# A small unread transfer as the first issue, and the first y load behind the opening barrier

## The chip, the cores and the metric

The kernel runs on one core of a Trainium2 chip. The metric is the device time of one execution in microseconds, the median of several. The span in a profile runs from the first instruction that the profile keeps to the last, and is some 1.6 us shorter than the device time. All runs told here were at a granted clock of 1.0; the program uses no TensorE.

## The reference

```python
x, y: 1024 x 4096 float32
return np.sum(np.abs(x - y), axis=-1)     # 1024 sums
```

33.55 MB are read and 4 KB are written.

## The kernel before

Each of the 128 partitions holds eight rows. Four rows of x (`xa`) and four of y (`yb`) come first, then three more rows of x (`xb`), then y rows into the places of `yb` that the subtractions have left free, and the last row in five pieces. VectorE subtracts in place, and ScalarE takes the absolute value and sums it with one instruction. The helper `put` places an instruction in the program's opening block. With `before="Drain"` it stands ahead of the issuing engine's part of the opening barrier, otherwise behind it.

```python
for r in (slice(0, 1), slice(1, H)):                     # SP, ahead of the barrier
    put(lambda: nc.sync.dma_start(out=xa[:, r, :], in_=xr[:, r, :]).then_inc(s_first, 16), before="Drain")
put(lambda: nc.scalar.dma_start(out=yb, in_=yr[:, 0:H, :]).then_inc(s_first, 16), before="Drain")   # ACT
put(lambda: nc.sync.dma_start(out=xb[:, 0:H - 1, :], in_=xr[:, H:K - 1, :]).then_inc(s_xb, 16))     # behind it
for k in range(H - 1):
    put(lambda: nc.sync.wait_ge(s_sub, k + 1))           # the subtraction of row k has freed yb[k]
    put(lambda: nc.sync.dma_start(out=yb[:, k, :], in_=yr[:, H + k, :]).then_inc(s_row[k], 16))
...                                                      # the last row, in pieces
# VectorE: the first subtraction waits for s_first >= 48, that is for all of xa and yb
...
put(lambda: nc.sync.wait_ge(s_end, n_part + 3))
put(lambda: nc.sync.dma_start(out=orr, in_=ro).then_inc(s_out, 16))
```

## Time and profile before

| | kernel before |
|---|---|
| device time, median of 6 beside the changed kernel | 84.59 us (84.42 to 84.68) |
| span of the profiled execution (84.33 us) | 82.7 us |
| DMA engines at work, mean of 16 | 95.6% of the span |
| VectorE, ScalarE busy | 44%, 38% |
| VectorE's first wait for data ends | 41.0 us |
| last reduction starts | 80.77 us |

The table says that the transfers bound the kernel: no compute engine is busy for half of the span. The views that show it, and the first microseconds in which the change acts, stand in the prediction. The end of the timeline of the kernel before (start us, length us, engine, line, what, and in brackets the idle time ahead and its releaser):

```profile
80.27 0.46 DVE L161 TENSOR_TENSOR last_piece<-xb_rows,yb_rows 128x288 f32<-128x288 f32 x1 [0.20 <-DMA yb_rows<-in_y_dram]
...
80.77 0.46 DVE L163 TENSOR_REDUCE ro_sums<-last_piece 128x1 f32<-128x292 f32 x1
```

The last subtraction starts when the last piece of y is there, and the reduction follows it directly. So the end hangs on the end of the stream.

### The profile page before, as it was taken

What the parts mean: (1) busy time and instruction counts of PE and PEld (TensorE: products, weight loads), DVE (VectorE), ACT (ScalarE), POOL (GpSimd) and SP (SyncE); (2) the same over time, 40 slices, a digit from 0 to 9 for tenths busy, and PEclk for the clock granted to TensorE, in tenths of its full rate; (3) what the DMA queues carried; (4) which work ended last, traced back from release to release, by engine and by line L of the source; (5) the groups of instructions that cost most, each with busy time, mean ns of one, the idle gap of its engine ahead of it and who ended that gap; (6) DMA issues with size and microseconds to landing.
All of it is one profiled execution on the core that took longest, in us unless ns stands there. A gap on an engine that the chain in (4) does not pass through costs nothing.

```text
span 82.7 us, 104 instructions
## 1 busy us (share of the span) xinstructions
DVE 36.3 (44%) x16; ACT 31.6 (38%) x27; POOL 0.2 (0%) x4
## 2 busy tenths in 40 slices
DVE  0000000000000000000199999999279898999682
ACT  3200000000000000000000979889790599999990
POOL 0000000000000000000000000000000000000000
DMA  4990992992998889988888999858999989999950
GB/s 127 634 634 24 610 634 87 547 634 127 507 507 380 380 380 547 594 380 380 380 380 380 452 618 452 380 254 380 483 404 436 452 380 431 414 411 413 404 209 2
DMA packets 2592, 33.56 MB, mean 406 GB/s; under 512 B 416, under 2 KB 928, under 8 KB 1696
## 3 DMA queue, kind: packets, MB, share of 16 engines
q1 hardware_dynamic: 2448, 25.17, 72.2%
q10 hardware_dynamic: 144, 8.39, 23.4%
HBM read 33.55 MB, written 0.00 MB: 406 GB/s over the span
## 4 chain that ended last, share of the span: by engine, by line
DMA 68%; DVE 22%; ACT 7%; ACTq 0%; SPq 0%; issue 0%
DMA xa_rows<-in_x_dram 49%; DMA yb_rows<-in_y_dram 19%; DVE xa_rows L127 16%; ACT xb_rows L132 7%; DVE xb_rows L127 5%; DVE ro_sums L163 1%; ACTq L199 0%; SPq L106 0%
## 5 line engine op out<-in xcount | busy, mean ns | idle before, releaser
L127 DVE TENSOR_TENSOR xa_rows<-xa_rows,yb_rows 128x4096 f32<-128x4096 f32 x4 | 17.4, 4420 | 41.0 <-DMA xa_rows<-in_x_dram 41.0
L132 ACT ACTIVATE xa_rows<-xa_rows 128x4096 f32<-128x4096 f32 x4 | 14.5, 3617 | 44.8 <-DVE xa_rows L127 44.8
L127 DVE TENSOR_TENSOR xb_rows<-xb_rows,yb_rows 128x2048 f32<-128x2048 f32 (+5 forms) x9 | 17.9, 2019 | 3.6 <-DMA yb_rows<-in_y_dram 3.5
L132 ACT ACTIVATE xb_rows<-xb_rows 128x2048 f32<-128x2048 f32 (+5 forms) x9 | 15.2, 1686 | 3.1 <-DVE xb_rows L127 3.0
L132 ACT ACT_TABLE_LOAD x1 | 1.3, 1283 | 1.3 <-PEq L185 1.3
L132 ACT ACTIVATION_READ_ACCUMULATOR xb_rows<-xb_rows 128x1 f32 x9 | 1.7, 186 | 0.0
L132 ACT ACTIVATION_READ_ACCUMULATOR xa_rows<-xa_rows 128x1 f32 x4 | 0.7, 186 | 0.0
L161 DVE TENSOR_TENSOR last_piece<-xb_rows,yb_rows 128x288 f32<-128x288 f32 x1 | 0.5, 458 | 0.2 <-DMA yb_rows<-in_y_dram 0.2
L163 DVE TENSOR_REDUCE ro_sums<-last_piece 128x1 f32<-128x292 f32 x1 | 0.5, 456 | 0.0
L155 DVE TENSOR_REDUCE ro_sums<-half_sums 128x2 f32<-128x4 f32 x1 | 0.1, 149 | 0.0
L185 POOL MEMSET const-bfloat16-1.0<- 128x1 bf16 x1 | 0.1, 101 | 0.0
L185 POOL MEMSET const-uint8-127<- 128x1 uint8 x1 | 0.1, 101 | 0.0
L185 POOL MEMSET const-float32-0.0<- 128x1 f32 x1 | 0.1, 98 | 0.2 <-issue 0.2
L185 POOL MEMSET const-float32-1.0<- 128x1 f32 x1 | 0.1, 98 | 0.0
## 6 DMA issues: line engine op xcount, KB each, us to landing
xa_rows<-in_x_dram SPq DMA_DIRECT2D x1, 6144.0 KB, 40.6
xb_rows<-in_x_dram SPq DMA_DIRECT2D x1, 6144.0 KB, 54.3
yb_rows<-in_y_dram SPq DMA_DIRECT2D x3, 2048.0 KB, 15.5
xa_rows<-in_x_dram SPq DMA_DIRECT2D x1, 2048.0 KB, 24.0
xb_rows<-in_x_dram SPq DMA_DIRECT2D x1, 864.0 KB, 17.8
yb_rows<-in_y_dram SPq DMA_DIRECT2D x1, 864.0 KB, 16.0
xb_rows<-in_x_dram SPq DMA_DIRECT2D x1, 528.0 KB, 16.9
yb_rows<-in_y_dram SPq DMA_DIRECT2D x1, 528.0 KB, 17.7
```

Source lines behind the costliest of these rows:

```text
L127: put(lambda: nc.vector.tensor_sub(out=tx, in0=tx, in1=ty).then_inc(s_sub, 1))
L132: put(lambda: nc.scalar.activation(tx, tx, ABS, accum_out=to).then_inc(sem, 1))
L155: put(lambda: nc.vector.reduce_sum(out=ro[:, K - 3:K - 1], in_=half, axis=AX).then_inc(s_end, 1))
L161: put(lambda: nc.vector.tensor_sub(out=last[:, n_part:n_part + w], in0=tx, in1=ty).then_inc(s_end, 1))
L163: put(lambda: nc.vector.reduce_sum(out=ro[:, K - 1:K], in_=last, axis=AX, apply_absolute_value=True).then_inc(s_end, 1))
L185: nc = _bacc.Bacc("TRN2", target_bir_lowering=False, num_devices=1)
```

## The change

The intent, as one reads it from the code, is to wake the DMA path with a transfer that nobody reads, so that the first large transfer behind it finds the path ready. It puts one descriptor of 512 bytes on each of the 16 DMA engines. At the same time ACT's y transfer moves behind the opening barrier.

```diff
+    probe = sbuf("probe", [16, 128])
+    s_probe = tc.alloc_semaphore("s_probe")
...
+    put(lambda: nc.sync.dma_start(out=probe, in_=xr[0:P:P // 16, 0, 0:128]).then_inc(s_probe, 16), before="Drain")
     for r in (slice(0, 1), slice(1, H)):
         put(lambda: nc.sync.dma_start(out=xa[:, r, :], in_=xr[:, r, :]).then_inc(s_first, 16), before="Drain")
-    put(lambda: nc.scalar.dma_start(out=yb, in_=yr[:, 0:H, :]).then_inc(s_first, 16), before="Drain")
+    put(lambda: nc.scalar.dma_start(out=yb, in_=yr[:, 0:H, :]).then_inc(s_first, 16))
...
+    put(lambda: nc.sync.wait_ge(s_probe, 16))
     put(lambda: nc.sync.wait_ge(s_end, n_part + 3))
```

## The prediction

> **What bounds the kernel now.** I read the page's queue part first, then the chain that ended last, then the first microseconds of the timeline, and last the same stretch by quarter microseconds. One row of the strip in slices and the two DMA queues of the kernel before:
>
> ```profile
> DMA  4990992992998889988888999858999989999950
> ...
> q1 hardware_dynamic: 2448, 25.17, 72.2%
> q10 hardware_dynamic: 144, 8.39, 23.4%
> ```
>
> The columns of the queues are packets, MB and share of 16 engines' time. 72.2% and 23.4% are 95.6% of the span of 82.7 us, so each of the 16 DMA engines is at work for 79.1 us. q1 holds what SP issues, q10 the one 8.39 MB y transfer that ACT issues. VectorE is busy 44% and ScalarE 38%. The chain of waits says the same (start us, us, what):
>
> ```profile
> 0.43 40.55 DMA xa_rows<-in_x_dram
> ...
> 41.00 13.11 DVE xa_rows L127 x3
> ...
> 54.13 16.08 DMA yb_rows<-in_y_dram
> ...
> 74.76 5.47 ACT xb_rows L132 x8
> ...
> 80.77 0.46 DVE ro_sums L163
> ```
>
> VectorE waits until 41.0 us for the first 16.8 MB (four rows of x and of y per partition, counted by one semaphore to 48), and then again and again for y rows. The stretch 41.00 to 54.11 is put down to VectorE only because its subtractions free the buffers for the later y rows. The DMA strip stays near full there: 6 MB of x were already queued behind the first x rows and keep the engines fed. So this is one gapless stream: about 1.0 us of start, 79.1 us of transfer, ending at 80.1 us, and VectorE's last wait for data indeed ends at 80.27 us. Then come the last subtraction (0.46 us), the last reduction and the store. ScalarE runs nearly without a gap from 64.98 to 80.75 us, so at the end it is almost level with the stream, but its work too comes at the stream's pace. Whatever moves the beginning of the stream moves the end by as much; whatever only changes the order in which x and y share the engines moves nothing, as long as there is always something queued.
>
> The timeline of the first microseconds (start, length, engine, line, what) is where the change acts:
>
> ```profile
> 0.00 0.85 SPq L106 DMA_DIRECT2D xa_rows<-in_x_dram  x2
> 0.12 0.36 ACTq L107 DMA_DIRECT2D yb_rows<-in_y_dram  x1
> ...
> 1.26 1.28 ACT L132 ACT_TABLE_LOAD   x1 [1.26 <-PEq L185]
> 1.26 0.33 SPq L108 DMA_DIRECT2D xb_rows<-in_x_dram  x1
> ```
>
> One issue occupies its sequencer for 0.33 to 0.47 us (SP's two are 0.38 by the chain and the rest of 0.85). The barrier lets SP and ACT go at 1.26 us, about 0.4 us after SP's second issue ended. Now the same stretch in windows; the last two columns are the DMA share and GB/s, and a packet is booked whole in the window in which it starts, which the shares above 1 show:
>
> ```profile
> 1.00:1.25 0.25, 0.00 (x0) 0.00 (x0) 0.00 (x0) 1.00 2.83 655
> 1.25:1.50 0.25, 0.00 (x0) 0.24 (x1) 0.00 (x0) 1.00 1.08 328
> 1.50:1.75 0.25, 0.00 (x0) 0.25 (x1) 0.00 (x0) 1.00 0.22 66
> 1.75:2.00 0.25, 0.00 (x0) 0.25 (x1) 0.00 (x0) 1.00 0.00 0
> 2.00:2.25 0.25, 0.00 (x0) 0.25 (x1) 0.00 (x0) 1.00 0.96 393
> 2.25:2.50 0.25, 0.00 (x0) 0.25 (x1) 0.00 (x0) 1.00 1.59 655
> 2.50:2.75 0.25, 0.00 (x0) 0.04 (x1) 0.00 (x0) 1.00 0.60 262
> 2.75:3.00 0.25, 0.00 (x0) 0.00 (x0) 0.00 (x0) 1.00 7.31 3146
> ...
> 5.10:5.60 0.50, 0.00 (x0) 0.00 (x0) 0.00 (x0) 1.00 1.22 524
> ...
> 5.74:6.20 0.46, 0.00 (x0) 0.00 (x0) 0.00 (x0) 1.00 5.26 2280
> ```
>
> An x packet of the first row is 16,384 bytes (one row of one partition), a y packet 65,536. 655 GB/s in 0.25 us is 10 x packets, then 5, then 1: the first packet on each of the 16 engines. Their shares add to 4.13, times 0.25 us: 1.03 us for each. The next sixteen (6 and 10) take (0.96 + 1.59) x 0.25 = 0.64 us each. In the settled stream sixteen x packets take 1.22 x 0.50 = 0.61 us each and sixteen y packets 5.26 x 0.46 = 2.42 us. So the first packet of each engine costs some 0.42 us more than a settled one. That is the only idle that a small transfer ahead could hide. It is also seen that y, although ACT issued it at 0.12 us, has its first packet only at 2.5 to 3.25 us, after two x packets on each engine.
>
> **What the Trainium skill says.** "DMA: Bandwidth & Descriptors", Queues, rings and completion order, says that each DMA engine takes turns between the queues with work for it, a packet at a time. The trace agrees: at 5.1 us sixteen x packets, at 5.74 us sixteen y packets, and so on. The same page, Issuing engines are not separate DMA queues, says transfers issued by different engines run on the same 16 DMA engines and interleave, and that issuing from several only saves sequencer time; the two queue shares that add to 95.6% of the same engines agree. Its section Latency and other measured facts gives about 600 ns to the first byte for such transfers; here the first issue ends at 0.38 us and the first packets start just after 1.00 us, which is 0.62 us and agrees, for the earliest engines. Its section on why a DMA increments its semaphore by 16 says that the number of engines used follows from the slowest dimension, here 16 on both sides: the small transfer then puts one 512-byte descriptor on each of the 16 engines. No run so far shows that for this shape.
>
> **The change part by part.** First, the small transfer. It moves 8 KB of 33.55 MB; at 406 GB/s (the page's mean) that is 0.02 us. Its issue is one SP instruction ahead of the first x row, an estimated 0.35 us from the 0.33 to 0.38 us above. The mean start of the first x packets, with windows counted at their middles, is (10 x 1.125 + 5 x 1.375 + 1 x 1.625) / 16 = 1.23 us, and their mean end 1.23 + 1.03 = 2.26 us. After the change they should start at 1.23 + 0.35 = 1.58 us. If the small transfer has taken the cold start upon itself, they take 0.62 us (between the 0.61 and 0.64 above) and end at 2.20 us: 0.06 us sooner than now. If each new transfer pays anew, they take 1.03 us and end at 2.61 us: 0.35 us later.
>
> Second, y behind the barrier. SP now has three issues ahead of its part of the barrier, so the release should move from 1.26 to about 1.61 us; ACT issues y then. With the same delay as the first x row, from issue to the mean first packet 1.23 us, y packets start near 2.84 us, against 2.5 to 3.25 us now. x fills the engines until then, with 32 packets' worth per engine queued in SP's first two row transfers, so no idle arises: x gains at most a packet or so of 0.61 us ahead of y and y loses as much. y landed at 0.12 + 28.1 = 28.2 us and the first x rows at 40.98 us, so y has 12.8 us to spare before the wait at 41.0. The cost on the path is 0. The table load on ACT begins some 0.7 us later (0.35 and the issue of 0.36), ahead of ScalarE's first work at 45.46 us: 0.
>
> Third, the wait for the small transfer before the store. SP waits there already, as its own queue of waits shows (us in total, times, longest):
>
> ```profile
> SPq L167 <- DVE ro_sums L163: 12.0, 1, 12.0
> ```
>
> The new wait passes at once inside those 12.0 us: 0. The xb issue behind the barrier, 0.35 us later, stands behind 8 MB of x: 0.
>
> The sum is between -0.06 and +0.35 us, all from the start of the stream.
>
> **The rivals.** (1) The cold start is paid once and the small transfer hides it. For it speaks that the second packets already took 0.64 us. It makes -0.06 us, or up to -0.2 us if ACT's issue at 0.12 us, now out of the way, had slowed SP's first transfer too. (2) The delay belongs to every transfer that finds its engines idle, or to fetching each transfer's own descriptors; then the issue is simply added, +0.35 us. Against it: later transfers show no such cost, but they come while the engines are busy, so the trace can't decide. (3) Something upsets the even interleaving: y starts so late that the x queue runs dry, or the engines' offsets at the start (second packets begin 2.00 to 2.50 us) widen and every landing waits for the slowest. The queued 8 MB of x speaks against the first; the second could be worth 0.2 us either way. (4) A large gain from x getting all engines at the start: the first wait needs both x and y, so it gains nothing.
>
> **Range and chances.** I give (1) about two thirds and (2) about one third: 0.67 x -0.1 + 0.33 x 0.35 is about +0.05 us. I take +0.07, hence 84.70 us. The runs before lie between 84.5 and 84.68 us; with the extremes of the mechanisms, -0.3 and +0.4 us, the range is 84.35 to 85.10. Two per cent would be 1.69 us, twenty-four times the shift that I expect and over four times the largest that I can work out; either verdict but "same" is left one chance in a hundred.
>
> **What would show it.** The small transfer's packets should start near 1.0 us, x packets at 1.3 to 1.9 us. Their length decides between (1) at 0.6 us and (2) at 1.0 us. The barrier should release near 1.6 us, the first y packet start at 2.6 to 3.3 us, VectorE's first wait end at 40.9 to 41.4 us, and every later wait and the end shift by the same amount as that one. The queue shares should stay near 79.1 us of work per engine. I would be wrong if VectorE's first wait moved by over 0.5 us, if a gap opened in the DMA strip, or if the packets settled at another pace than 0.61 and 2.42 us.

## The result, and the profile after

The changed kernel takes 84.93 us (median of 6, 84.87 to 85.11), beside 84.59 us (84.42 to 84.68) for the kernel before. The ratio is 1.0044, with a 95% interval of 1.0029 to 1.0059. A ratio is the mean time of one kernel's fast runs over that of the other's of the same rounds, so it is not quite the ratio of the medians. The difference of the means is 84.95 - 84.58 = 0.38 us. The verdict is "same" at 2%, but the loss is clear of the noise.

The queues and the DMA strip of the changed kernel (packets, MB, share of 16 engines):

```profile
DMA  6897999798979989499888899858999989999950
...
q1 hardware_dynamic: 2480, 25.18, 72.0%
q10 hardware_dynamic: 144, 8.39, 23.2%
```

The shares add to 95.2% of 83.4 us, which is 79.4 us of work per engine, against 79.1 us before. The strip is again full from its second slice to the end. The stream has not become slower. It begins later, as the chain of waits (start us, us, what) shows:

```profile
1.73 39.88 DMA yb_rows<-in_y_dram
...
41.64 13.11 DVE xa_rows L131 x3
...
54.76 16.06 DMA yb_rows<-in_y_dram
...
75.38 5.47 ACT xb_rows L136 x8
...
81.38 0.46 DVE ro_sums L167
```

Against the chain of before, VectorE starts 0.64 us later (41.64 against 41.00), the next wait 0.63 us (54.76 against 54.13), ScalarE's last run 0.62 us and the last reduction 0.61 us. So everything that is lost is lost ahead of the first subtraction, and nothing is given back or added behind it. The two profiled executions took 84.99 and 84.33 us, so 0.66 us apart, more than the 0.38 us of the means. The profiled execution of before was faster than any of its six timed runs. A second pair of profiles, told below, is 0.55 us apart.

The first microseconds of the changed kernel's timeline:

```profile
0.00 0.38 SPq L108 DMA_DIRECT2D probe<-in_x_dram  x1
...
0.44 0.89 SPq L110 DMA_DIRECT2D xa_rows<-in_x_dram  x2
1.73 0.33 SPq L112 DMA_DIRECT2D xb_rows<-in_x_dram  x1
1.73 0.37 ACTq L111 DMA_DIRECT2D yb_rows<-in_y_dram  x1
```

The small transfer takes SP as long to issue as the 2 MB transfer did (0.38 us), and the first x row follows at 0.44 us where it stood at 0 before. The barrier opens at 1.73 us instead of 1.26. Now the windows, in which a packet is booked whole where it starts (the last two columns are the DMA share and GB/s):

```profile
1.00:1.25 0.25, 0.00 (x0) 0.00 (x0) 0.00 (x0) 1.00 0.11 27
1.25:1.50 0.25, 0.00 (x0) 0.00 (x0) 0.00 (x0) 1.00 0.91 203
1.50:1.75 0.25, 0.00 (x0) 0.00 (x0) 0.00 (x0) 1.00 3.49 721
1.75:2.00 0.25, 0.00 (x0) 0.00 (x0) 0.00 (x0) 1.00 0.56 131
...
2.50:2.75 0.25, 0.00 (x0) 0.25 (x1) 0.00 (x0) 1.00 0.55 197
2.75:3.00 0.25, 0.00 (x0) 0.25 (x1) 0.00 (x0) 1.00 1.83 786
3.00:3.25 0.25, 0.00 (x0) 0.25 (x1) 0.00 (x0) 1.00 0.15 66
```

27 GB/s in 0.25 us is 13 packets of 512 bytes, and the 203 GB/s after it are the other three and three x packets. Then come 11 and 2 x packets, the first on each engine. Their shares from 1.25 us on add to 4.96, times 0.25: 1.24 us for each of the sixteen (the small packets in it are 0.025 us each). The second sixteen, 3 and 12 and 1, start between 2.5 and 3.25 us, where before they started between 2.0 and 2.5 us. This is the reading that decides between the rivals of the prediction. In the packet records the last small packet ends at 1.36 us and the first x packet starts at 1.48 us: the small transfer had come and gone on every engine, and the first x packets still took 1.23 us on average (1.24 by the windows) and not 0.62.

From the packet records of the trace, the first sixteen x packets, one for each engine, end at 2.26 us on average before and at 2.85 us after: 0.59 us later. I call this mean end T below. It measures the beginning of the stream well, because from there on the start of a packet meets the end of another one in the records. (The records do not name the engine; that each has one of the first sixteen packets is read from this pattern.) Of the 0.59 us, 0.39 are a later start of these packets (1.62 against 1.23 us) and 0.20 their greater length.

A warning on one name in the chain. It says that VectorE waited for y, and gives y 39.88 us to landing. The queue of y in the stretch from 36 to 42 us says something else (packets, MB, share of that stretch):

```profile
q1 hardware_dynamic: 64, 2.36, 90.9%
q10 hardware_dynamic: 8, 0.00, 0.1%
```

y's queue moved no data any more, only eight completion writes; all the data there are SP's, which is x. In the records y's last data packet ends at 35.6 us and its last completion write starts at 37.4, while the last one of the first x rows starts at 41.2 us. The three transfers raise the same semaphore, and the profile seems to hand the counts to the transfers in the wrong order. That fits what the Trainium skill says in "DMA: Bandwidth & Descriptors", Why a DMA increments its semaphore by 16 and not by 1: with two transfers in flight on one semaphore, the count does not tell whose it is. The kernel is safe, because it waits for the full 48.

### The profile page after: what moved, and what is told of

Its sections match the earlier page's. It is cut to its first block, busy times and chain, and to the rows that moved or that the text cites. A ratio compares the mean times of both kernels' runs of the same rounds, so it can differ in the third digit from the quotient of the medians.

```text
span 83.4 us, 106 instructions
## 1 busy us (share of the span) xinstructions
DVE 36.3 (44%) x16; ACT 31.6 (38%) x27; POOL 0.2 (0%) x4
## 4 chain that ended last, share of the span: by engine, by line
DMA 67%; DVE 22%; ACT 7%; ACTq 0%; issue 0%
DMA yb_rows<-in_y_dram 67%; DVE xa_rows L131 16%; ACT xb_rows L136 7%; DVE xb_rows L131 5%; DVE ro_sums L167 1%; ACTq L204 0%
```

## The experiments

The theories were these. **I**: every issue that SP makes ahead of the first x row is added to the start; the cold first packets stay as they are, and where y is issued does not matter. **II**: part of the loss comes from y not being at the engines in the first microseconds. **III**: the small transfer does warm the path, but the effect is hidden by something else. The twelve runs went in three groups of four, each group on one chip with runs of the kernel before among them. "Mean difference" is against the runs of before of the same group, and T is from the profile of the run. The diffs of p2, p7 and p11 are against the kernel before, the others against the changed kernel. They are shortened: the sizes of the buffer `probe` and the count of its wait go with them and are left out where they add nothing.

| run | first x row issued at us | T us | T minus issue | mean difference us | ratio, 95% interval |
|---|---|---|---|---|---|
| before, first profile | 0 | 2.26 | 2.26 | - | - |
| changed kernel | 0.44 | 2.85 | 2.41 | +0.38 | 1.0044 (1.0029 to 1.0059) |
| p1_probe_only | 0.43 | y came first | - | +0.28 | 1.0032 (1.0011 to 1.0053) |
| p2_y_moved_only | 0 | 2.34 | 2.34 | -0.09 | 0.9990 (0.9965 to 1.0015) |
| p3_probe_on_act | 0 | 2.28 | 2.28 | -0.01 | 0.9997 (0.9973 to 1.0021) |
| p4_two_probes | 0.88 | 3.30 | 2.42 | +0.91 | 1.0106 (1.0084 to 1.0127) |
| p5_probe_12k | 0.44 | 3.50 | 3.06 | +1.29 | 1.0149 (1.0124 to 1.0174) |
| p6_probe_12k_wait | 3.53 | 5.83 | 2.30 | +3.66 | 1.0431 (1.0399 to 1.0464) |
| p7_useful_first | 0, in columns | other packets | - | +0.29 | 1.0033 (1.0010 to 1.0055) |
| p8_before_again | 0 | 2.28 | 2.28 | -0.12 | 0.9985 (0.9964 to 1.0005) |
| p9_probe_spread | 0.61 | 3.19 | 2.58 | +0.91 | 1.0106 (1.0074 to 1.0138) |
| p10_probe_behind | 0 | 2.39 | 2.39 | +0.07 | 1.0007 (0.9976 to 1.0038) |
| p11_useful_halves | 0, in halves | 2.69 | 2.69 | +0.24 | 1.0025 (0.9991 to 1.0060) |
| p12_after_again | 0.43 | 2.78 | 2.35 | +0.46 | 1.0053 (1.0022 to 1.0085) |

### p1_probe_only: the small transfer without moving y

```diff
-    put(lambda: nc.scalar.dma_start(out=yb, in_=yr[:, 0:H, :]).then_inc(s_first, 16))
+    put(lambda: nc.scalar.dma_start(out=yb, in_=yr[:, 0:H, :]).then_inc(s_first, 16), before="Drain")
```

> The small transfer first on SP, y still issued by ACT ahead of the barrier as in the kernel before. Theory I (each issue ahead of the first x row is added to the start, the cold first packets cost the same as ever, where y is issued does not matter): +0.35 to +0.45 us against before, first x packets last about 1.0 us. Theory II (part of the loss is y's absence: the first x packets lasted 1.23 us on average instead of 1.03 because no y was at the engines): +0.15 to +0.25 us, first x packets back at about 1.0 us. Theory III (the small transfer hides the start once y is in place): 0 or less.

The median was 84.89 us against 84.61, a mean difference of +0.28 us. That lies between what I wrote for I and for II, and the trace tells why neither reading fits. ACT issued y at 0.12 us and SP the first x row only at 0.43 us, so y came first at the engines. Its first packets lasted 2.90 us on average instead of 2.42, so the cold start of 0.48 us was then y's. The time does not separate the two theories. III falls: with y in its old place the small transfer still loses. One thing stays unexplained here: y is wanted data too and was issued at 0.12 us, so if the time of the first wanted issue were all, about 0.12 us would be lost. But y's first packets started 1.41 us after their issue on average (1.54 us), where those of x before started after 1.23 us, and VectorE's first wait ended at 41.35 us against 41.00 and 41.04 us in the two profiles of before. So a small transfer ahead of y on another queue went with a later start of y; no run separates why.

### p2_y_moved_only: y behind the barrier without the small transfer

```diff
-    put(lambda: nc.scalar.dma_start(out=yb, in_=yr[:, 0:H, :]).then_inc(s_first, 16), before="Drain")
+    put(lambda: nc.scalar.dma_start(out=yb, in_=yr[:, 0:H, :]).then_inc(s_first, 16))
```

> No small transfer; y issued by ACT behind the barrier. Theory I: 0 within 0.1 us, the first x packets start at 1.0 to 1.5 us and last about 1.03 us as before; y's first packets come after two or three x packets. Theory II: +0.15 to +0.25 us, the first x packets last about 1.2 us. If ACT's early issue had slowed SP's (the small gain in the prediction): -0.1 us.

84.48 us against 84.61, a mean difference of -0.09 us, with an interval that holds 1. Theory II is refuted as far as the time goes. The first x packets did last longer (1.17 us against 1.03, and 1.12 in p8), as II had it, but they started sooner (1.17 against 1.23 us on average) and ended at 2.34 us, only 0.08 us later. The length alone misleads; the end counts. One line of the expectation was wrong: y's first packets came after many more than two or three x packets, at 4.9 to 6.2 us.

### p3_probe_on_act: the small transfer issued by ACT

```diff
-    put(lambda: nc.sync.dma_start(out=probe, ...).then_inc(s_probe, 16), before="Drain")
+    put(lambda: nc.scalar.dma_start(out=probe, ...).then_inc(s_probe, 16), before="Drain")
```

> The small transfer is ACT's first issue, ahead of the barrier; SP's issues are those of before; y behind the barrier on ACT. Theory I: the first x row is issued at 0 again, so 0 to +0.1 us against before. Theory II: as y moved alone, +0.15 to +0.25 us. If the small transfer itself makes the following packets slower (they lasted 1.23 us behind it): about +0.2 us with x packets near 1.2 us though x is issued at 0.

84.53 us against 84.61, a mean difference of -0.01 us. All the instructions of the change are there, but SP's first issue is x again, at 0, and with one issue less on SP the barrier opens at 1.24 us as before; p10 takes these two apart. The loss is gone. Here the small packets reached the engines at 2.8 to 3.1 us, behind two x packets, so this run says nothing on warming. It says that the small transfer as such costs nothing that these times show.

### p4_two_probes: two small transfers on SP

```diff
-    put(lambda: nc.sync.dma_start(out=probe, in_=xr[0:P:P // 16, 0, 0:128]).then_inc(s_probe, 16), before="Drain")
+    for h in (0, 1):
+        put(lambda: nc.sync.dma_start(out=probe[:, 128*h:128*h+128], in_=xr[0:P:P // 16, 0, 128*h:128*h+128]).then_inc(s_probe, 16), before="Drain")
```

> Two small transfers first on SP, y behind the barrier. Theory I: one more issue of about 0.44 us, so 0.8 us against before (0.4 us more than the changed kernel's 0.37 us). Theory III (a warm-up that came too late or too small with one): no more, or less, than the changed kernel. Theory II: the same 0.44 us more as theory I, so this run does not separate those two, but it gives the price of an issue alone.

85.47 us against 84.61, a mean difference of +0.91 us, so about twice the loss with one, as theory I has it. The timeline and the windows of this kernel:

```profile
0.00 0.84 SPq L109 DMA_DIRECT2D probe<-in_x_dram  x2
...
0.88 0.90 SPq L111 DMA_DIRECT2D xa_rows<-in_x_dram  x2
...
1.40:1.90 0.50, 0.00 (x0) 0.00 (x0) 0.00 (x0) 1.00 0.07 17
1.90:2.70 0.80, 0.00 (x0) 0.12 (x1) 0.00 (x0) 1.00 1.39 328
```

x is issued at 0.88 us: two issues at a pitch of 0.44 us. The window up to 1.90 us holds the second small transfer's sixteen packets. The next one holds the first sixteen x packets, 1.39 x 0.80 = 1.11 us each. A second small transfer directly ahead warms no more than the first.

### p5_probe_12k and p6_probe_12k_wait: was 512 bytes too little, and is the start paid once?

```diff
-    put(lambda: nc.sync.dma_start(out=probe, in_=xr[0:P:P // 16, 0, 0:128]).then_inc(s_probe, 16), before="Drain")
+    put(lambda: nc.sync.dma_start(out=probe, in_=xr[0:P:P // 16, 0, 0:3072]).then_inc(s_probe, 16), before="Drain")
+    put(lambda: nc.sync.wait_ge(s_probe, 16), before="Drain")        # p6 alone
```

12 KiB are three quarters of a row. The buffer `probe` is made larger to match, on the same 16 partitions.

> The changed kernel with a probe of 12 KiB on each engine in place of 512 bytes (0.46 us of settled stream, three quarters of 0.61). Theory A (the cold start is paid once, by the first transfer of any volume; 512 bytes were too few): the probe's packets last 0.8 to 1.1 us, the x row's first ones behind it 0.61 to 0.65 us, and the time is +0.46 us against before, all of it the added data. Theory B (a fixed delay of about 1.65 us from a transfer's issue to its data, after which packets stream; a transfer that comes while the engines work hides it): the same lengths, +0.44 to +0.5 us. The two part in the next run. If neither holds and the x row still pays behind 12 KiB: its packets 1.0 us or more and +0.8 us or more.

> SP waits for the 12 KiB probe to land before it issues the first x row, so the engines are idle again but no longer cold. Theory A: the first x packets last 0.61 to 0.65 us and end 1.7 to 1.9 us after their issue. Theory B: they last 1.0 to 1.25 us and end 2.2 to 2.5 us after their issue, as in every run so far. The time is about 2 to 2.5 us above before in either case (the landing of the probe, some 2.3 us).

p6 took 88.07 us against 84.43, a mean difference of +3.66 us; I had written 2 to 2.5 us, because I had taken the landing of the 12 KiB to be 2.3 us and it was 3.5. The question of the run is answered all the same. Its timeline and windows around the first x row:

```profile
3.53 0.82 SPq L111 DMA_DIRECT2D xa_rows<-in_x_dram  x2
...
4.40:4.65 0.25, 0.00 (x0) 0.00 (x0) 0.00 (x0) 1.00 2.76 590
4.65:5.00 0.35, 0.00 (x0) 0.00 (x0) 0.00 (x0) 1.00 1.46 328
```

590 GB/s in 0.25 us are 9 packets and 328 GB/s in 0.35 us are 7. Their length is 2.76 x 0.25 + 1.46 x 0.35 = 1.20 us, although every engine had already moved 12 KiB by 2.24 us. They end 2.30 us after their issue, as the first packets of a cold kernel do. **So the start is not paid once in a kernel: after a pause of 2.3 us it came back in full.** Theory A is refuted and the first half of B holds.

p5 took 85.73 us against 84.43, +1.29 us, where both A and B had about +0.46. The third reading that I had written down came out: behind engines that had 12 KiB to do, the first x packets still lasted 1.50 us. So the second half of B, that a working engine hides the delay, did not show. The landing of the 12 KiB, 3.8 us here, raised a suspicion against the experiment itself. All engines write into 16 neighbouring partitions. The Trainium skill, "SBUF — State Buffer", Door 1: The DMA port swizzle, gives a map by which partitions 0 to 15 lie on 4 of 16 ports, and 27.2 GB/s for each port. An estimate from that: 196.6 KB / (4 x 27.2 GB/s) = 1.8 us instead of 0.46. Hence p9.

### p9_probe_spread: the same 12 KiB on partitions four apart

```diff
-    probe = sbuf("probe", [16, 3072])
+    probe = sbuf("probe", [P, 1536])
-    put(lambda: nc.sync.dma_start(out=probe, in_=xr[0:P:P // 16, 0, 0:3072]).then_inc(s_probe, 16), before="Drain")
+    put(lambda: nc.sync.dma_start(out=probe[0:P:4, :], in_=xr[0:P:4, 0, 0:1536]).then_inc(s_probe, 16), before="Drain")
```

> The 12 KiB per engine of the earlier run, now on 32 partitions four apart (two descriptors of 6 KiB for each engine) in place of 16 neighbouring partitions. If that run's excess (+1.25 us where the added data are 0.46 us) came from all engines writing into 16 neighbouring partitions: the probe's packets last about 0.23 us after the first, the first x packets 0.61 to 0.7 us, and the time is +0.45 to +0.6 us. If every transfer's first packets pay even behind a busy engine: x packets of 1.0 us or more, and +0.9 us or more.

85.44 us against 84.42, a mean difference of +0.91 us. The transfer now landed after 2.6 us instead of 3.8, which fits the page's map. The windows:

```profile
1.60:1.87 0.27, 0.00 (x0) 0.00 (x0) 0.00 (x0) 1.00 0.39 137
1.87:2.72 0.85, 0.00 (x0) 0.28 (x1) 0.00 (x0) 1.00 1.35 381
```

The second window holds the last ten 6 KiB packets and the sixteen first x packets. In the packet records these x packets last 1.00 us on average. So part of p5's excess was the narrow destination, and part was not: the x row pays even behind a working engine. The second reading of the expectation holds. T is 2.58 us after the issue of x, later than the 2.26 to 2.42 us on idle engines. There is a side effect that I had not reckoned with. The issue itself took 0.55 us in this form, and x followed at 0.61 us.

### p10_probe_behind: the small transfer behind SP's two x issues

```diff
-    put(lambda: nc.sync.dma_start(out=probe, ...).then_inc(s_probe, 16), before="Drain")
     for r in (slice(0, 1), slice(1, H)):
         put(lambda: nc.sync.dma_start(out=xa[:, r, :], ...).then_inc(s_first, 16), before="Drain")
+    put(lambda: nc.sync.dma_start(out=probe, ...).then_inc(s_probe, 16), before="Drain")
```

> The changed kernel with the 512-byte transfer moved behind SP's two x issues, still ahead of the barrier: barrier, y and table load are as late as in the changed kernel, x is issued at 0. If the loss is the first wanted data issued 0.44 us later: 0 within 0.1 us. If part of it is the later barrier and y (1.7 us): +0.2 us or more, which would also explain the +0.28 us of the run with the first row cut in columns.

The mean difference is +0.07 us, ratio 1.0007 with an interval of 0.9976 to 1.0038; the medians, 84.62 and 84.42 us, differ by 0.20, because three of the eleven runs of before that stood beside it took longer (84.74 to 85.06). The timeline shows that everything else of the change is as late as in the changed kernel:

```profile
0.00 0.84 SPq L109 DMA_DIRECT2D xa_rows<-in_x_dram  x2
...
0.88 0.43 SPq L110 DMA_DIRECT2D probe<-in_x_dram  x1
1.72 0.38 ACTq L111 DMA_DIRECT2D yb_rows<-in_y_dram  x1
```

The barrier opens at 1.72 us and y is issued then. T is 2.39 us, against 2.78 us in the changed kernel run beside it (p12). Against p12 itself p10 is 0.39 us faster in the mean (six runs of 84.53 to 84.70 us against six of 84.93 to 85.06). So the place of the small transfer ahead of x makes most of the loss. A part from the later barrier is not excluded: T is 0.11 us later than in p8, and the interval against before reaches +0.32 us.

### p7_useful_first and p11_useful_halves: a third issue that carries wanted data

```diff
-    for r in (slice(0, 1), slice(1, H)):
-        put(lambda: nc.sync.dma_start(out=xa[:, r, :], in_=xr[:, r, :]).then_inc(s_first, 16), before="Drain")
+    for r, c in ((slice(0, 1), slice(0, 1024)), (slice(0, 1), slice(1024, C)), (slice(1, H), slice(0, C))):          # p7
+        put(lambda: nc.sync.dma_start(out=xa[:, r, c], in_=xr[:, r, c]).then_inc(s_first, 16), before="Drain")
+    for p, r in ((slice(0, P, 2), slice(0, 1)), (slice(1, P, 2), slice(0, 1)), (slice(0, P), slice(1, H))):          # p11
+        put(lambda: nc.sync.dma_start(out=xa[p, r, :], in_=xr[p, r, :]).then_inc(s_first, 16), before="Drain")
```

VectorE then waits for 64 in place of 48, and y is behind the barrier in both.

> No probe: the first x row is cut in columns, 1024 and 3072, so that SP has three issues ahead of the barrier as in the changed kernel, but the first one carries 2 MB/4 of wanted data, 1.2 us of work per engine; y behind the barrier. If any third issue costs its 0.44 us: +0.4 us. If what counts is when the first wanted data is issued: 0 within 0.1 us.

> The first x row cut by partitions, the even ones first, then the odd ones, in whole 16 KiB packets; three issues ahead of the barrier, y behind it. If the +0.28 us of the run with columns came from its small packets at the start: 0 to +0.1 us. If any further issue among the first ones costs: +0.25 us or more.

p7 lost 0.29 us where I expected 0. Part of it is measured: in the settled stream a 4 KiB packet takes 0.159 us and a 12 KiB packet 0.460, together 0.008 us more than the 0.611 of a whole row, which over eight rows per engine is 0.06 us. Another part is at the start: 32 KiB per engine are done at 3.06 us on average, against 2.90 before. (0.05 us of these 0.16 are again the greater length of the eight 4 KiB packets, so the parts must not simply be added.) p11 was to separate the small packets from the further issue, and it is inconclusive. Its ratio of 1.0025 has an interval from 0.9991 to 1.0060, and its own first issue took 0.55 us instead of 0.38, so its first packets start only at 1.33 us. Both runs issue wanted data at 0 and still lost 0.29 and 0.24 us, the second within its noise. Whether a further issue with wanted data can be free at the start stays open. What neither run shows is a gain.

### p8_before_again and p12_after_again: the controls

p8 is the kernel before without an edit, and p12 the changed kernel without an edit.

> The kernel before itself, as a control of the measure and for a second profile: ratio 1.000 within 0.002; first x packets end 2.2 to 2.4 us after the span's start on average; a span of 82.7 to 83.0 us, since the profiled run of before was its fastest of seven.

> The changed kernel itself beside the same runs of before, with a second profile: +0.37 us within 0.1 us (ratio 1.003 to 1.0055); first x packets start near 1.6 us and end 2.7 to 2.9 us on average. It tells whether the 0.66 us between the two profiled spans is the draw of those two executions.

p8 came out at 0.9985 (0.9964 to 1.0005): a kernel against itself can differ by 0.12 us, so nothing under about 0.15 us is argued from times here. p12 gave 1.0053 (1.0022 to 1.0085), a mean difference of +0.46 us, the size of the first measurement within that noise. The profiled executions of p8 and p12 took 84.38 and 84.93 us, 0.55 us apart, with T at 2.28 and 2.78 us. So the 0.66 us between the first two profiles was in part the draw. No run beat the kernel before by more than the control did, so there is no better version to show.

## Why the prediction was right or wrong, point by point

- **What bounds the kernel: right.** A shift at the beginning of the stream appeared at VectorE's first wait, at every later wait and at the end with the same 0.61 to 0.64 us. Over the runs with whole 16 KiB first packets, T against its 2.27 us of before gives the time: +1.03 for +0.91 us (p4), +1.23 for +1.29 (p5), +3.56 for +3.66 (p6), +0.92 for +0.91 (p9), +0.07 for -0.09 (p2), +0.01 for -0.01 (p3), +0.12 for +0.07 (p10). It gives too much for the changed kernel itself (+0.58 for +0.38, in p12 +0.51 for +0.46) and for p11 (+0.42 for +0.24); one profile is one draw, and I have no other reason for these.
- **The choice between the rivals: this is the step that failed.** The prediction gave (1), "The cold start is paid once and the small transfer hides it", about two thirds. The first x packets behind the small transfer lasted 1.24 us, not the 0.62 us of (1). p4 shows that a second small transfer changes nothing, p6 that the cost returns on engines that have already worked, and p9 that it is there even on engines at work. What (2) said, "the issue is simply added", is close to what the runs show, with +0.35 us where +0.38 us was measured (+0.46 in p12). Its "transfer that finds its engines idle" is too narrow: p5 and p9 paid behind engines at work, 1.50 and 1.00 us. Its other wording, the fetching of each transfer's own descriptors, was not tested. The stated centre of 84.70 us was low by 0.23 us because of that weight. (Its weighted sum gives +0.05 us and it took +0.07; its extremes around 84.63 us give 84.33 to 85.03 us and it wrote 84.35 to 85.10.) The range held because it was drawn around both rivals, not because the favoured one was right.
- **A sign of being wrong came true.** The prediction named a move of VectorE's first wait "by over 0.5 us". It moved by 0.64 us (41.00 to 41.64) in the first pair of profiles and by 0.52 us (41.04 to 41.56) in p8 and p12. The span named for its end, "40.9 to 41.4 us", was missed in both. The other two signs, a gap in the strip and another pace of the packets, did not appear.
- **The size of the issue: too small.** "An estimated 0.35 us" was the busy length of an issue. The pitch from one issue to the next, which is what delays x, is 0.44 us (0.383 us of issue and 0.056 us to the next). The packets of x were also not at their old length, as (2) had reckoned with 1.03 us, but at 1.23 us (1.16 in p12), so T moved by 0.59 us (0.50 between p8 and p12) and not by 0.35.
- **y behind the barrier costs 0: right, by reasoning that was partly wrong.** p2 and p3 show no cost. But y's first packets did not start near 2.84 us. They started at 5.3 to 6.6 us, since each engine first served several more x packets. y did not lose "at most a packet or so". Its last data ended at 35.6 us instead of 26.1, because it now shared the engines with the 48 KiB packets of the later x rows. 9.5 of its margin of "12.8 us" went. I take the cost to have stayed 0 because VectorE needs both x and y, and their sum is what the engines moved; that is argued and not tested apart.
- **The release at "about 1.61 us"** was 1.73 us, again the pitch of the issue. The table load at 2.13 us and the new wait ahead of the store cost nothing, as said: ScalarE's first work came at 46.10 us, and SP still waited 10.5 us for the last reduction.
- **What stays open.** The runs show that the first packets of x, in a plain issue, end 2.26 to 2.42 us after the start of the transfer's own issue when the engines are idle, and not earlier when they are at work (2.58 and 3.06 us in p9 and p5). They don't show what fills that time. That a small packet lasts only 0.025 us in the same phase, that the first x packets lasted 1.23 us in the changed kernel and 1.16 in p12 where they lasted 1.03 and 1.12 us in the two profiles of before, and that issues in p9 and p11 took 0.55 us or more, is measured and not explained.

## What to carry to other kernels

Before adding a warm-up transfer, measure whether the start-up belongs to the kernel or to the transfer: let the engines work, let them fall idle, and issue again. If the second start costs the same, as here, a transfer issued ahead does not pre-pay it, and then it counts how early the first wanted transfer is issued. In this stream without gaps, each small transfer ahead of SP's first x row cost about the pitch of its issue (+0.38 to +0.46 us for one, +0.91 for two), and the same issue behind it or on ACT cost nothing that could be measured (+0.07 and -0.01 us). An early first issue is not all: p1, p7 and p11 had wanted data issued at 0 or 0.12 us and were still 0.24 to 0.29 us slower (p11 within its noise).

## What the Trainium skill lacked or had wrong

- "DMA: Bandwidth & Descriptors", Latency and other measured facts: the 600 ns to the first byte agree with the first packet's start (0.62 us after the end of the issue), but the first 16 KiB packets are done only 2.26 to 2.42 us after the start of their issue, where the settled length of a packet is 0.61 us. No page gives the length of a transfer's first data packets.
- No page says that the first data packets last longer, or whether earlier work of the engines shortens them. (A fixed cost for every transfer is stated, "SBUF — State Buffer", The DMA setup-cost knee; that page puts it mostly into the completion, while here the data packets themselves are late.) Earlier work did not bring them near the settled 0.61 us: 1.20 us for the first packets after a pause (p6), 1.00 us behind working engines (p9), 1.03 to 1.12 us in the two profiles of the kernel before.
- "DMA: Bandwidth & Descriptors", Issuing engines are not separate DMA queues, calls the sequencer's time for an issue usually small relative to the transfer. Here it is 0.38 us for 8 KB as for 2 MB, with a pitch of 0.44 us, and ahead of the first wanted transfer that is about what the change cost (+0.38 and +0.46 us).
- The same page, Queues, rings and completion order: the taking of turns is seen in the settled stream, one x and one y record at a time, but a queue that joins later waits for more than one record. y started at 4.9 to 6.6 us, having been issued at 1.3 to 1.7 us (p2, the changed kernel). By the page a packet holds several descriptors; how many of them one record of the trace is, no run shows, so this need not contradict the page.
- No page gives issue lengths by form. Issues into partitions that are two or four apart, and the first plain one behind them, took 0.55 to 0.59 us instead of 0.37 to 0.43 (p9, p11).
